# A decoder step's FFN on Trainium2: the first two pairs of gate/up feature tiles without combined products, slice roles, and the place of one down weight

## The chip, the cores and the metric

The kernel runs on one core of a Trainium2 chip. The metric is the device time of one execution in microseconds (us), the median over several runs. The engines are named as in the profile: PE (TensorE), DVE (VectorE), ACT (ScalarE), POOL (GpSimd) and SP (the queue that issues most of the DMAs).

## The reference, cut to what matters

The reference is one inference step of a two-layer decoder: an mLSTM layer, then an attention layer, each followed by a SwiGLU FFN. The change is inside the FFN, which runs twice (once a layer):

```python
def swiglu(xn, w_gu, w_d):
    gu = xn @ w_gu
    return (jax.nn.silu(gu[..., :D_FF]) * gu[..., D_FF:]) @ w_d

h = h + swiglu(rmsnorm(h, prm['norm_ffn'][l]), prm['w_gate_up'][l], prm['w_down'][l])
```

`D_MODEL` is 1024 and `D_FF` is 2816. There are 1104 tokens (64 of the sample group, 16 meta tokens and 1024 of the prompt); both groups use the same weights. All inputs are float32.

## The kernel before, in words

**Precision.** Each float32 operand is split into a high and a low part (`hi` by a cast on ACT, `lo` by a subtraction on DVE; `Net.split`, L330 and L331, and the same two steps in `PairWeights.split`, L114 and L115, and in `Mix.cast` and `Mix.rest`). A product is three matmuls: hi x hi, hi x lo, lo x hi (`mm3`, or the loop at L1326).

**Token slices.** The tokens are three slices `t` = 0, 1, 2 of 336, 384 and 384 columns. Activations lie feature-major in `H[t]`: partitions are 128 features, then 8 feature blocks, then the tokens of the slice. `y(k, t)` is block pair `k` (256 features, 768 columns of 384) of slice `t`.

**Order of an FFN.** `mlp` first runs the layer's output projection, slice after slice (`unit(t, m, x)`, tiles `pops`): 24 matmuls for each of 8 output blocks, an add into `H` on DVE (L529), a square on ACT and a running sum of squares (`add_sq`, L403) on POOL or DVE, and a write of `H` to memory (`hD`). While slice 2 is projected, the slices before it are normalised (`Mix.zero` for slice 0, `Mix.one` for slice 1) and the first weights are prepared. Then `ffn` runs gate/up, then down.

**Gate/up.** The 22 tiles of 128 features of gate and up are taken two at a time as 22 `Unit(x)`: even `x` is a pair of gate tiles, odd `x` the matching pair of up tiles. A pair of feature tiles, four blocks of the contraction and three token slices would be 24 block products; the kernel makes 20, numbered `r` = 0 to 19, from sums and differences of weight blocks (`SUMS`, made on POOL by `PairWeights.sums`, L99) and of activation blocks (made once for all units from the `y(k, t)`). Each product is 6 matmuls on PE (`u.p(r, b)`, accumulating in PSUM bank `b`). Products in `PURE` (0, 2, 11, 15) have 336 columns, the others 384. Intermediate bank contents are copied out on ACT (`u.copy`, L1332) or added to or subtracted from a saved part on DVE (`u.mark`, L1306 and L1307). `u.out(c, i, t)` ends an output tile: for a gate pair a Silu on ACT (L1348), kept in place; for an up pair a multiply with the kept tile on DVE (L1345) and a write to memory (`hT`, L1346, issued on SP). The parts are called `s1`, `c15`, `s2`, `e`, `t4`, `v2`; `fs` gives each two places, for even and odd units; `swap` exchanges two pairs of places in every second even unit, because a kept gate tile is still needed while the next gate pair begins. A unit's last four products (19, 14, 6, 3) are issued inside the next unit, interleaved with its first ones (`steps(u, v)`), so product 6 of unit `x` marks the same place of each following unit.

Raw weights come in by `weights.load(x)` (L75, on SP), one unit's pair at a time. Sums for unit `x + 1` are made while unit `x` runs.

**The first unit** (`x` = 0) is written out by hand in `ffn` from L1459 on: its products stand between the steps that normalise slice 2 (`m.root(2)`: a matmul of the sums of squares and a square root; `m.inverse(2)`: three reciprocals; `scaled` on DVE, `times` on POOL) and combine the slices (`m.add`, `m.sub` on DVE or, with `True`, on POOL; `m.cast` and `m.rest` into the operand tiles). Its raw weights and some sums lie in the `ny` tile, its sums are made during slice 2's projection.

**Who sets the order.** Inside `manual_schedule` the named engines keep program order: PE always, DVE and ACT too from slice 2's projection to L1566 and again from the last gate/up unit on (L1583). POOL and SP are ordered by the framework's planner, as are DVE and ACT in the steady units.

**Down.** The chunks `seq` go over slice `t`, half `z` of the output and 11 pairs `c` of hidden tiles, with 24 matmuls each (`dps`). Each chunk needs a weight block (`w_load(i)`, L1450, 512 KB into one of three places, `slots[0]`, `slots[1]` and `wr`, in turn; `w_split(i)`) and, for `z` = 0, a hidden block (`h_load(j)`, L1433, on POOL; `h_split(j)`). `wr` belongs to a pool that is opened only when the gate/up pool is closed. `H` itself is reloaded from `hD` by L1647.

Of the kernel before, what the change touches and what calls it, by code (L numbers as in the profile page):

```python
# [7 lines left out]
F32 = mybir.dt.float32  # L8
# [38 lines left out]
BLOCKS = ((17, 15, 18, 10), (8, 2, 9, 13), (12, 5, 1, 4), (11, 0, 14, 7), (6, 3))  # L47
SAME = {16: 4, 19: 14}
STAGED = (15, 18, 10, 2, 9, 13, 12, 5, 1, 4, 11, 0, 14, 6)
# [3 lines left out]
        (5, (1, 0), (1, 1), 1), (4, (1, 2), (1, 3), 1), (11, 9, (0, 3), -1), (0, (0, 1), (1, 1), -1), (14, (0, 2), (0, 3), 1),  # L53
        (6, (0, 0), (0, 1), 1))
# [3 lines left out]
class PairWeights:  # L58
# [3 lines left out]
    def __init__(self, net, w, slots, H, first):  # L62
        self.net, self.w, self.H, self.first, self.slots = net, w, H, first, slots
        self.both = [(slots[2 + g], slots[LOW[g]]) for g in range(4)]
        self.at = {r: (g, i) for g, b in enumerate(BLOCKS) for i, r in enumerate(b)}

    def raw(self, x, f, k, n=1):
        at, o = ((self.first, 0), (self.H[0], 0), (self.H[1], 0))[0 if x == 0 else 1 + x % 2]
        o += f * KT * P + k * 2 * P
        return at[:, o : o + n * 2 * P]  # L70
# [6 lines left out]

    def place(self, r, n=1, low=True):
        g, i = self.at[r]
        return self.both[g][low][:, i * 2 * P : (i + n) * 2 * P]  # L80

    def staged(self, x, r):
        last = (4, 11, 0, 6, 14, 5)
        if x == 0 and r in (1, 3):
            return (self.first, 8) if r == 1 else (self.slots[1], 3)
        i = last.index(r) if x == 0 and r in last else STAGED.index(r)
        return (self.slots[i // 4], i % 4) if i < 8 else (self.H[2], i - 8)

    def source(self, x, r, n=1):
        if isinstance(r, tuple):  # L90
            return self.raw(x, *r)
        if r in SINGLE and (x or r != 3):
            return self.raw(x, *SINGLE[r])
        t, i = self.staged(x, r)
        return t[:, i * 2 * P : (i + n) * 2 * P]

    def sums(self, x, part=slice(None)):
        for o, a, b, s in SUMS[part]:
            self.net.nc.gpsimd.tensor_tensor(out=self.source(x, o), in0=self.source(x, a), in1=self.source(x, b),  # L99
                                             op=ALU.add if s > 0 else ALU.subtract)  # L100

    def split(self, x, g, only=None):
        runs = []
        for r in BLOCKS[g]:
            if only and r not in only:
                continue
            at = self.staged(x, r) if r in STAGED else None
            if at and runs and runs[-1][2] and runs[-1][2][0] is at[0] and runs[-1][2][1] + runs[-1][1] == at[1]                     and self.at[runs[-1][0]][1] + runs[-1][1] == self.at[r][1]:
# [3 lines left out]
        for r, n, _ in runs:  # L112
            hi, lo, src = self.place(r, n, False), self.place(r, n), self.source(x, r, n)
            self.net.nc.scalar.copy(hi, src)  # L114
            self.net.nc.vector.tensor_tensor(out=lo, in0=src, in1=hi.bitcast(F32), op=ALU.subtract)  # L115
# [5 lines left out]
class Mix:  # L121
# [3 lines left out]
    def __init__(self, net, H, g, pp):  # L125
        self.net, self.nc, self.H, self.g, self.pp = net, net.nc, H, g, pp
        self.X = {}
# [43 lines left out]
    def gained(self, t, k):  # L171
        y = self.H[t][:, k, : TS[t][1] - TS[t][0]]
        self.nc.scalar.activation(y, y, AF.Copy, scale=self.net.gain[:, self.g + k : self.g + k + 1])

    def times(self, t, k):
        y = self.y(k, t, self.n)
        self.nc.gpsimd.tensor_tensor(out=y, in0=y, in1=self.r.unsqueeze(1).broadcast_to([P, 2, self.n]), op=ALU.mult)
# [5 lines left out]
    def zero(self, two):  # L183
# [3 lines left out]
        v = [t[:, : 2 * n].rearrange("p (k n) -> p k n", k=2) for t in two]  # L187
# [4 lines left out]
        self.places(self.net.new_x(0), PURE)  # L192
        for k in (2, 1, 3, 0):
            self.scaled(0, k)
            yield
            if k == 2:
                self.cast(15, y(2))
            elif k == 1:
                self.add(v[0], y(1), y(2))
                self.cast(0, v[0])  # L200
                self.rest(15, y(2))
            elif k == 3:
                self.cast(11, y(3))
                self.rest(0, v[0])
            else:
                self.add(v[1], y(0), y(3))
                self.cast(2, v[1])
            yield
        self.rest(11, y(3))
        self.rest(2, v[1])  # L210

    def one(self):
# [4 lines left out]
        self.places(self.net.new_x(1), (4, 14, 13, 3))  # L217
        self.scaled(1, 2)
        yield
        self.scaled(1, 3)  # L220
        self.cast(4, y(2, 1))
        self.scaled(1, 1)
        self.cast(14, y(3, 1))
        self.scaled(1, 0)
        yield
        self.rest(4, y(2, 1))
        self.sub(y(1, 0), y(1, 1), y(1, 0))
        self.sub(y(2, 0), y(1, 0), y(2, 0))
        yield
        self.rest(14, y(3, 1))  # L230
        self.cast(13, y(2, 0))
        self.sub(y(2, 1), y(2, 1), y(3, 1))
        self.add(y(3, 1), y(2, 0), y(2, 1))
        self.cast(3, y(3, 1))
        yield
        self.rest(13, y(2, 0))
        self.sub(y(2, 0), y(0, 1), y(0, 0), True)
        yield
        self.rest(3, y(3, 1))
        self.sub(y(3, 1), y(2, 0), y(3, 0), True)  # L240
        self.sub(y(2, 1), y(3, 1), y(2, 1), True)


class Net:
# [219 lines left out]
    def mlp(self, H, w, l, heads=None, cb=None):  # L464
# [8 lines left out]
        with self.pool(self.uid("nsp")) as sp, self.pool(self.uid("npp"), bufs=2, space=PSUM) as pn:  # L473
# [26 lines left out]
            with ExitStack() as c:  # L500
# [24 lines left out]
                def unit(t, m, x):  # L525
# [4 lines left out]
                    self.add_sq(H, t, m, sp, x, KT - 1 if t < 2 else KT - 2)  # L530
                    (nc.sync if t == 2 else nc.gpsimd).dma_start(self.hD[:, m, TS[t][0] : TS[t][1]], H[t][:, m])

                weights = PairWeights(self, self.I["w_gate_up"][l], slots, flat, nyt.rearrange("p x k n -> p (x k n)"))
# [2054 lines left out]
```

## Time and profile before

| | |
|---|---|
| median of 3 runs | 3036.09 us (3033.24 to 3036.29) |
| profiled execution: time, span | 3033.08 us, 3031.4 us |
| mean granted PE clock | 0.976 |
| busy share of the span | PE 94%, DVE 57%, ACT 43%, POOL 37% |
| gate/up of layer 0: first matmul of unit 0 to last of unit 21 | 577.65 to 1083.15 us |
| gate/up of layer 1 | 2228.35 to 2732.17 us |

A row of a timeline gives the start in us from the span's start, the duration in us, the engine, the line of the kernel, the operation, `output<-inputs` by tile names, the shape, and in brackets the idle time of that engine before it and what ended the idle time. `x3` means that three such instructions in a row were merged. Matmul durations overlap, since a matmul is issued before the one ahead of it has ended: how fast PE works is seen from the distance of their starts. In a row of waits, the numbers are the total in us, how often, and the longest. In layer 0 the tiles of `H` appear as `vA`, in layer 1 as `Ht`; the twelve-odd tiles called `slot` hold raw weights, sums and split weights in turn.

### The profile page before, as it was taken

The numbers are of one execution on the slowest core, as the hardware profiler recorded it, in microseconds if no ns is written. First come the engines' busy times: TensorE is split into PE (matmuls) and PEld (weight loads), VectorE is DVE, ScalarE is ACT, GpSimd is POOL, SyncE is SP. The second block draws the span as 40 slices with busy tenths as digits, with TensorE's granted clock in tenths as the row PEclk, the third lists the DMA queues.
The fourth block names the chain that finished last, engine by engine and source line by source line (L and its number), as shares of the span: only waits on it lengthen the run. The fifth ranks groups of instructions, "written<-read, shape, count | busy, mean of one in ns | idle before, by whom it ended". The sixth has DMA issues, their size and how long they took to land.

```text
span 3031.4 us, 53802 instructions
## 1 busy us (share of the span) xinstructions
PE 2836.8 (94%) x20446; PEld 2694.8 (89%) x20446; DVE 1721.3 (57%) x3462; ACT 1314.0 (43%) x2627; POOL 1117.5 (37%) x1644
## 2 busy tenths in 40 slices
PE   7999988789999989999999999999969999998999
PEld 7998878779999989999999887676968999998998
DVE  5032555877776745463355443776487667764543
ACT  5122453344444434342344444777234444443432
POOL 2011224565655511104353101544447565631110
PEclk9999999899999999999999999999989999999999
DMA  7052535122222266544443675442412222226653
GB/s 219 15 128 81 138 101 190 43 78 79 74 74 74 88 222 209 182 142 149 132 165 133 229 273 210 135 144 81 152 52 70 73 80 79 74 86 228 207 186 105
DMA packets 300142, 392.81 MB, mean 130 GB/s; under 512 B 32238, under 2 KB 222698, under 8 KB 298858
## 3 DMA queue, kind: packets, MB, share of 16 engines
q1 hardware_dynamic: 262978, 270.05, 27.5%
q0 software_dynamic: 33232, 117.01, 11.7%
q8 instruction: 161, 2.64, 0.4%
q10 hardware_dynamic: 3672, 2.31, 0.3%
q14 instruction: 99, 0.81, 0.1%
HBM read 292.19 MB, written 97.10 MB: 128 GB/s over the span
## 4 chain that ended last, share of the span: by engine, by line
PE 63%; DVE 14%; ACT 5%; issue 4%; DMA 3%; POOL 1%; DVEq 0%; ACTq 0%; POOLq 0%; SPq 0%
PE m L1326 21%; PE dps L261 6%; PE dps L260 6%; PE dps L262 6%; PE tmps L260 3%; PE tmps L261 3%; PE tmps L262 3%; DVE slot L115 2%; PE sp L2375 1%; PE op L2462 1%; DVE s L2379 1%; PE pops L262 1%; PE pops L260 1%; PE pops L261 1%; ACT slot L114 1%
## 5 line engine op out<-in xcount | busy, mean ns | idle before, releaser
L1326 PE MATMUL m<-x2h,slot 128*128 128x384 f32 x704 | 205.2, 342 | 27.5 <-ACT x2h L140 23.6
L1326 PE MATMUL m<-x0h,slot 128*128 128x336 f32 x704 | 186.2, 319 | 1.1 <-ACT vA L1332 0.5
L331 DVE TENSOR_TENSOR slot<-slot,slot 128x1024 fp32r<-128x1024 f32 x96 | 123.2, 1288 | 100.6 <-ACT slot L330 100.4
L115 DVE TENSOR_TENSOR slot<-slot,slot 128x512 fp32r<-128x512 f32 (+2 forms) x184 | 142.3, 780 | 53.4 <-ACT slot L114 47.9
L403 POOL TENSOR_TENSOR ns<-ns,nq 128x384 f32<-128x384 f32 (+1 forms) x70 | 77.8, 1111 | 235.7 <-ACT nq L401 234.2
L330 ACT CAST slot<-slot 128x1024 fp32r<-128x1024 f32 x96 | 100.8, 1052 | 144.7 <-PE dps L261 105.6
L1326 PE MATMUL m<-x1h,slot 128*128 128x384 f32 x528 | 158.8, 341 | 0.4 <-DVE vA L529 0.4
L1326 PEld LDWEIGHTS m<-x2h,slot 128*128 128x128 f32 x704 | 131.4, 191 | 30.2 <-ACT x2h L140 24.2
L114 ACT CAST slot<-slot 128x512 fp32r<-128x512 f32 (+2 forms) x184 | 111.5, 614 | 103.2 <-PE m L1326 95.3
L115 DVE TENSOR_TENSOR slot<-Ht,slot 128x256 fp32r<-128x256 f32 (+2 forms) x105 | 91.3, 870 | 83.1 <-ACT slot L114 83.1
L115 DVE TENSOR_TENSOR slot<-vA,slot 128x256 fp32r<-128x256 f32 (+2 forms) x105 | 90.2, 860 | 83.7 <-ACT slot L114 83.7
L1433 POOL DMA_DIRECT2D hr<-hT x60 | 32.6, 543 | 275.5 <-DVE T_2l L331 75.5
L1326 PEld LDWEIGHTS m<-x0h,slot 128*128 128x128 f32 x704 | 125.9, 189 | 2.8 <-ACT c L1332 1.1
L99 POOL TENSOR_TENSOR slot<-vA 128x256 f32<-128x256 f32 x105 | 92.7, 899 | 90.4 <-DMA vA<-in_w_gate_up 88.5
L99 POOL TENSOR_TENSOR slot<-Ht 128x256 f32<-128x256 f32 x105 | 91.3, 886 | 92.2 <-DMA Ht<-in_w_gate_up 90.2
L1326 PE MATMUL m<-T_2h,slot 128*128 128x384 f32 x352 | 107.9, 347 | 17.9 <-ACT fs L1332 5.1
L1326 PE MATMUL m<-x2l,slot 128*128 128x384 f32 x352 | 120.0, 341 | 3.6 <-DVE x2l L136 3.6
L1326 PE MATMUL m<-T_4h,slot 128*128 128x384 f32 x352 | 108.2, 348 | 9.6 <-DVE Ht L1306 5.0
L1326 PE MATMUL m<-x0l,slot 128*128 128x336 f32 x352 | 112.0, 318 | 0.0
L331 DVE TENSOR_TENSOR slot<-wr,slot 128x1024 fp32r<-128x1024 f32 x44 | 56.7, 1289 | 80.1 <-ACT slot L330 77.1
L1326 PEld LDWEIGHTS m<-x1h,slot 128*128 128x128 f32 x528 | 98.5, 190 | 1.5 <-issue 0.7
L2402 ACT ACTIVATE s<-s,nb 128x272 f32<-128x272 f32 (+7 forms) x126 | 99.1, 788 | 0.0
(803 smaller groups left out, 10353.6 us busy)
## 6 DMA issues: line engine op xcount, KB each, us to landing
slot<-in_w_down SPq DMA_DIRECT2D x88, 512.0 KB
wr<-in_w_down SPq DMA_DIRECT2D x44, 512.0 KB
vA<-in_w_gate_up SPq DMA_DIRECT2D x42, 512.0 KB
Ht<-in_w_gate_up SPq DMA_DIRECT2D x42, 512.0 KB
hr<-hT POOLq DMA_DIRECT2D x46, 384.0 KB, 5.1
kp<-in_cache_k SPq DMA_DIRECT2D x32, 512.0 KB
vp<-in_cache_v SPq DMA_DIRECT2D x32, 512.0 KB
wraw<-in_w_in_a SPq DMA_DIRECT2D x24, 512.0 KB
```

The source lines that it names most:

```text
L99: self.net.nc.gpsimd.tensor_tensor(out=self.source(x, o), in0=self.source(x, a), in1=self.source(x, b), op=ALU.add if s > 0 else ALU.subtract)
L114: self.net.nc.scalar.copy(hi, src)
L115: self.net.nc.vector.tensor_tensor(out=lo, in0=src, in1=hi.bitcast(F32), op=ALU.subtract)
L260: mm(ps, sh, mh, start=first, stop=False)
L261: mm(ps, sh, ml, start=False, stop=False)
L262: mm(ps, sl, mh, start=False, stop=last)
L330: self.nc.scalar.copy(hi, src)
L331: self.nc.vector.tensor_tensor(out=lo, in0=src, in1=hi.bitcast(F32), op=ALU.subtract)
L403: (nc.vector if x >= late else nc.gpsimd).tensor_tensor(out=s, in0=s, in1=sq, op=ALU.add)
L1326: nc.tensor.matmul(u.b[b][:, :n], w[p][:, k], x[q][:, k], start=new and k == i == 0, stop=k == 1 and i == 2, skip_group_check=True)
L1433: nc.gpsimd.dma_start(hraw[j], hT[t][:, 2 * c : 2 * c + 2])
L2402: nc.scalar.activation(ss[z, u], ss[z, u], AF.Exp, bias=nb[:, z : z + 1], accum_out=sm[:, u, z : z + 1])
```

## The change

- **Two pairs plainly.** Units 0 and 1 (the first gate pair and its up pair) are no longer combined. `direct(x, t)` makes the two feature tiles of one pair and one slice by 2 x 8 x 3 plain matmuls, in the order (0, 0), (1, 0), (0, 1), (0, 2), (1, 1), (1, 2) of `(x, t)`. Their raw weights lie in `slots[0]` and `slots[1]` and are split whole (`plain_split`) during slice 2's projection. The combined units begin with `x` = 2, which so has no predecessor `v`.
- **Combinations behind them, without GpSimd.** `Mix.zero`, `Mix.one` and the hand-written part make the normalised slices first, then the sums and differences, all on DVE and ACT; `times` moves from POOL to DVE, and so do slice 2's sums of squares (`late` becomes 1). `load(2)` and `sums(2)` come when the combinations of slice 0 are done, since the raw weights overwrite it; `load(3)` later.
- **Slice roles.** `s2` and `e`, `s1` and `t4` exchange the slices 1 and 2 that they end in (`out`). `swap` becomes `turn`, a rotation of `s2`, `v2`, `e`, `t4` over four even units. `out("t4", ...)` moves behind the first `c15` mark.
- **Sums.** Two pairs of adds (5 and 4, 6 and 14) become one POOL instruction each, of 128 x 512.
- **Third raw down weight.** Chunk 2's raw weight goes to `flat[1]`, where the raw weights of unit 21 lay, and is loaded in unit 21's second step; `wr` is used from chunk 5 on.

```diff
-BLOCKS = ((17, 15, 18, 10), (8, 2, 9, 13), (12, 5, 1, 4), (11, 0, 14, 7), (6, 3))
+BLOCKS = ((17, 15, 18, 10), (8, 2, 9, 13), (12, 1, 5, 4), (14, 0, 11, 7), (6, 3))
...
-        (5, (1, 0), (1, 1), 1), (4, (1, 2), (1, 3), 1), (11, 9, (0, 3), -1), (0, (0, 1), (1, 1), -1), (14, (0, 2), (0, 3), 1),
-        (6, (0, 0), (0, 1), 1))
+        ((5, 4), 1), (11, 9, (0, 3), -1), (0, (0, 1), (1, 1), -1), ((6, 14), 0))
...
+    def plain_split(self, x, f):
+        self.net.split(self.raw(x, f, 0, 4), *self.plain(x, f))
...
     def times(self, t, k):
         y = self.y(k, t, self.n)
-        self.nc.gpsimd.tensor_tensor(out=y, in0=y, in1=self.r.unsqueeze(1).broadcast_to([P, 2, self.n]), op=ALU.mult)
+        self.nc.vector.tensor_tensor(out=y, in0=y, in1=self.r.unsqueeze(1).broadcast_to([P, 2, self.n]), op=ALU.mult)
...
-                    self.add_sq(H, t, m, sp, x, KT - 1 if t < 2 else KT - 2)
+                    self.add_sq(H, t, m, sp, x, KT - 1 if t < 2 else 1)
...
+                    if x > 1:
+                        mix.gained(2, rows[x - 2])
+                    if x in (2, 3):
+                        weights.plain_split(0, x - 2)
                     if x == 3:
...
+                        weights.load(1)
+                    if x in (5, 7):
+                        weights.plain_split(1, (x - 5) // 2)
...
-        swap = {"s2": "v2", "v2": "s2", "e": "t4", "t4": "e"}
+        turn = {"s2": "v2", "v2": "e", "e": "t4", "t4": "s2"}
...
-                u.at = {(swap.get(c, c) if x % 4 == 2 else c): p[x % 2] for c, *p in fs}
+                u.at = {}
+                for c in fs:
+                    o = c
+                    for _ in range(0 if u.odd else x // 2 % 4):
+                        o = turn.get(o, o)
+                    u.at[c] = fs[o][x % 2]
...
                 u.mark("t4", sub, 3, "t4")
-                u.out("t4", 1, 1)
                 u.p(11, 0)
                 u.mark("c15", add, 0, "c15", z)
+                u.out("t4", 1, 2)
...
-                wraw[i] = view((self.slots[0], self.slots[1], wr if i > 1 else None)[i % 3])
+                wraw[i] = view((self.slots[0], self.slots[1], wr if i > 2 else flat[1])[i % 3] if i > 1 else self.slots[i])
...
+        def direct(x, t):
+            n, ends = size[t], []
+            for f in range(2):
+                w = [a.rearrange("p (k n) -> p k n", k=KT) for a in weights.plain(x, f)]
+                b = bank("mp", "d")[:, :n]
+                for j in range(KT):
+                    k = 2 * (ks if t == 2 else (2, 1, 3, 0))[j // 2] + j % 2
+                    a = [z[:, k % 2] for z in m.X[m.D[t][k // 2]]]
+                    self.mm3(b, w[0][:, k], w[1][:, k], a[0], a[1], j == 0, j == KT - 1)
+
+                def evict(b=b, o=spare[t][f][:, :n], f=f):
+                    if x:
+                        tt(out=o, in0=b, in1=o, op=ALU.mult)
+                        nc.sync.dma_start(hT[t][:, f], o)
+                    else:
+                        nc.scalar.activation(o, b, AF.Silu)
+                ends.append(evict)
+            return ends
...
+        ends = direct(0, 0)
...
         m.root(2)
...
+        for evict in ends:
+            evict()
         m.inverse(2)
...
+        ends = direct(1, 0)
+        for i, k in enumerate(ks):
+            (m.scaled if k == last else m.times)(2, k)
+            m.cast_block(2, k)
+            if i:
+                m.rest_block(2, ks[i - 1])
+            if i == 2:
+                ends[0]()
+        m.rest_block(2, last)
+        ends[1]()
...
+        ends = direct(0, 1)
...
+        m.rest(9, y(0, 0), -1.0)
+        m.rest(13, y(2, 0), -1.0)
+        ends[1]()
         weights.load(2)
...
+        ends = direct(0, 2)
...
+        weights.sums(2)
...
+        ends = direct(1, 1)
+        weights.split(2, 0)
+        for evict in ends:
+            evict()
+        ends = direct(1, 2)
...
+        weights.load(3)
+        weights.split(2, 1)
+        ends[0]()
+        m.rest(19, y(3, 1))
+        weights.split(2, 4)
+        weights.split(2, 2)
+        ends[1]()
+        weights.sums(3, slice(0, 9))
         order.close()
         with fixed():
             v = None
-            for x in range(1, NF - 1):
+            for x in range(2, NF - 1):
...
                 if g == 1:
+                    w_load(2)
                     w_split(0)
...
-            for i in range(2, 5):
+            for i in range(3, 5):
                 w_load(i)
```

321 lines of the change are left out of this document (127 added, 194 removed).

## The prediction

> **What bounds the kernel now.** I read the page first, then the waits of TensorE over the whole span, then windows, timelines and the chain of waits around the places that these named.
>
> ```profile
> PE 2836.8 (94%) x20446; PEld 2694.8 (89%) x20446; DVE 1721.3 (57%) x3462; ACT 1314.0 (43%) x2627; POOL 1117.5 (37%) x1644
> PE m L1326 <- ACT x2h L140: 23.6, 2, 11.8
> PE dps L260 <- ACT x0h L330: 17.5, 2, 9.6
> PE nps L156 <- DVE ns L403: 14.8, 2, 8.1
> ```
>
> TensorE is the bound, and its three longest waits (us in total, times, longest) come once in each of the two layers' FFNs. Two are in the prelude, from the last output-projection matmul of token slice 2 (`pops`) into the gate/up units; one is at the start of the down projection. The prelude of layer 0:
>
> ```profile
> 576.87 0.34 PE L262 MATMUL pops<-x2h,wo 128*128 128x384 f32 x1
> 580.00:590.00 10.00, 2.01 (x4) 1.40 (x5) 7.32 (x10) 5.01 (x12) 4.64 (x3) 0.69 0.11 39
> 590.00:600.00 10.00, 5.97 (x23) 4.71 (x22) 9.87 (x10) 2.72 (x6) 4.30 (x2) 0.80 0.00 0
> 600.00:610.00 10.00, 0.69 (x1) 0.29 (x1) 9.83 (x7) 1.66 (x3) 7.51 (x3) 0.54 0.00 0
> 610.00:620.00 10.00, 8.62 (x32) 8.12 (x33) 6.64 (x8) 4.80 (x9) 1.20 (x2) 0.61 0.61 172
> 683.57 0.34 PE L1326 MATMUL m<-U_6h,wl0h 128*128 128x384 f32 x1
> 1044.18 0.34 PE L1326 MATMUL m<-U_6h,wl0h 128*128 128x384 f32 x1
> 2228.18 0.34 PE L262 MATMUL pops<-x2h,wo 128*128 128x384 f32 x1
> 2332.47 0.33 PE L1326 MATMUL m<-U_6h,wl1h 128*128 128x384 f32 x1
> ```
>
> Window columns are PE, PEld, DVE, ACT, POOL busy, granted clock, DMA share, GB/s. From 580 to 610 VectorE works 27 of 30 us and TensorE 9, and the granted clock falls to 0.54: slice 2's sum, norm and combinations are a serial DVE/POOL chain. The `U_6h` rows mark product 6 of the third unit, executed inside the fourth. So pops end (576.87+0.34) to that mark takes 106.4 us in layer 0 and 104.0 in layer 1. Seventeen units from 683.57 to 1044.18 take 21.2 us each.
>
> **Part 1, the first two pairs plainly.** What must TensorE do at least? The pitch of matmuls:
>
> ```profile
> 527.14 0.31 PE L262 MATMUL pops<-x0h,slot 128*128 128x336 f32 x1
> 529.92 0.32 PE L262 MATMUL pops<-x0h,slot 128*128 128x336 f32 x1
> 574.97 0.34 PE L260 MATMUL pops<-x2h,wo 128*128 128x384 f32 x1
> 576.87 0.34 PE L262 MATMUL pops<-x2h,wo 128*128 128x384 f32 x1
> ```
>
> Eighteen pitches of 336 columns lie between the first two rows (0.155 us each), eleven of 384 between the others (0.173). A combined unit has 20 products of 6 matmuls; a plain unit has 2 features x 3 slices x 8 x 3 = 144, 24 more, all of 336 columns. That costs 24 x 0.155 = 3.7 us, 14.9 us for four units in the two layers. To the mark the new kernel must issue: 288 plain matmuls (96 x 0.155 + 192 x 0.173 = 48.1), the third unit without a predecessor's tail (72 x 0.173 + 24 x 0.155 = 16.2), and seven products of the fourth (36 x 0.173 + 6 x 0.155 = 7.2): 71.5 us. Without stalls that is 34.9 and 32.5 us less than before.
>
> Which stalls remain? The plain order asks for slice 0, 0, 1, then 2, so slice 2's norm has 14.9+8.3 us of matmuls ahead of it. The chain on VectorE:
>
> ```profile
> 590.72 2.58 DVE L163 RECIPROCAL nr<-nr 128x128 f32<-128x128 f32 x3
> 593.43 4.30 POOL L177 TENSOR_TENSOR vA<-vA,nr 128x768 f32<-128x768 f32 x2 [8.71 <-issue]
> 596.09 2.45 DVE L133 TENSOR_TENSOR vA<-vA,vA 128x768 f32<-128x768 f32 x1
> 599.63 0.96 DVE L136 TENSOR_TENSOR vA<-vA,vA 128x768 f32<-128x768 f32 x1
> L331 DVE TENSOR_TENSOR slot<-slot,slot 128x1024 fp32r<-128x1024 f32 x96 | 123.2, 1288 | 100.6 <-ACT slot L330 100.4
> 612.55 26.34 SPq L75 DMA_DIRECT2D vA<-in_w_gate_up  x6
> 616.57 0.73 POOL L99 TENSOR_TENSOR slot<-vA 128x256 f32<-128x256 f32 x1 [7.50 <-DMA vA<-in_w_gate_up]
> 630.91 0.91 POOL L99 TENSOR_TENSOR vA<-slot,vA 128x256 f32<-128x256 f32 x1
> ```
>
> A 768-wide operation beside a GpSimd one took 2.45 us, without one 0.96. GpSimd's multiplies, subtractions and sums of squares move to VectorE, so the lengthening goes. In the slice-2 pass VectorE has about 11 768-wide operations, three reciprocals, four weight splits (1.29 each) and 15 evictions and sums of half a microsecond (0.55 in part 2's first row): 29 us beside 33 us of matmuls (192 x 0.173). I cost it at nothing: 7.4 us of slice 0's plain matmuls now stand between pops end and the root; with the old lag, the 8.1 us of the `nps` row, 0.7 would be left. After the root (about 9 us behind pops end: 7.4 of plain matmuls, root and square root) come the reciprocals (2.6), 20 operations of 768 at 0.92, and some 2 us of scaling and evictions before `load(2)` may overwrite slice 0: about 34 us behind pops end. In the old trace the fourteen sums ended 19.3 us after the load's issue (612.55 to 631.82), so the third unit's weights are whole at 53. TensorE arrives at 49. `split(2, 4)` needs the last sum and stands ahead of the unit's first eviction on ACT; TensorE has two products before it needs that eviction, and the splits take 2 more: a stall of about 5 us. With the root's matmul and a copy not covered by a tail, 7 us a layer. Bounds 3 (sums in 10 us) and 12 (chain 15% longer): 34.9 + 32.5 - 14 = **53 us gained** (43 to 61). `load(1)`, queued on SP behind an output write, holds later `hD` writes only, which nobody awaits; its splits stand on DVE ahead of later evictions, with three `po` buffers of slack.
>
> [...]
>
> **Part 2, slice roles and order of evictions.**
>
> ```profile
> 709.38 0.55 DVE L1345 TENSOR_TENSOR vA<-vA,vA 128x384 f32<-128x384 f32 x1
> 709.96 0.82 ACT L1332 COPY vA<-m 128x384 f32<-128x384 f32 x2 [0.59 <-DVE vA L1345]
> 710.50 0.44 PE L1326 MATMUL m<-T_2h,slot 128*128 128x384 f32 x1 [0.42 <-ACT vA L1332]
> 739.36 1.08 DVE L1345 TENSOR_TENSOR nr<-nr,vA 128x384 f32<-128x384 f32 x1
> 740.37 0.49 DVE L1306 TENSOR_TENSOR vA<-m,vA 128x336 f32<-128x336 f32 x1
> 740.91 0.45 PE L1326 MATMUL m<-T_4h,slot 128*128 128x384 f32 x1 [0.42 <-DVE vA L1306]
> ```
>
> Each steady unit has one idle of 0.42 us: in even units the `t4` copy awaits the multiply that frees its place, in odd ones product 19 awaits the `c15` add behind the `t4` multiply. The four-place rotation gives `t4` the place of the old `s2`, freed one multiply earlier; `out("t4")` goes behind the `c15` add. Nineteen units x 0.42 x 2 layers = 16; next late would be another copy, so I take **13** (-5 to 16). The fused adds (two of 128x512 for four of 128x256) do the same elements on a queue that runs ahead: nothing.
>
> **Part 3, the third raw down weight.**
>
> ```profile
> 1070.57 0.76 DVE L115 TENSOR_TENSOR wl0l<-vA,wl0h 128x256 fp32r<-128x256 f32 x2
> 1084.80 11.82 DMA wr<-in_w_down
> 1090.00:1095.00 5.00, 0.56 (x4) 0.28 (x2) 0.00 (x0) 0.00 (x0) 0.00 (x0) 1.00 1.03 407
> 1096.69 1.05 ACT L330 CAST slot<-wr 128x1024 fp32r<-128x1024 f32 x1 [18.43 <-DMA wr<-in_w_down]
> 1098.44 0.65 PE L260 MATMUL dps<-x0h,slot 128*128 128x336 f32 x1 [7.89 <-ACT x0h L330]
> 1100.00:1105.00 5.00, 5.00 (x18) 5.00 (x19) 4.86 (x6) 3.30 (x4) 1.46 (x2) 0.50 0.76 240
> 2733.82 13.51 DMA wr<-in_w_down
> slot<-in_w_down SPq DMA_DIRECT2D x10, 512.0 KB
> vA<-hD POOLq DMA_DIRECT2D x2, 1536.0 KB, 9.1
> ```
>
> The load into `wr` starts at 1084.80, takes 11.8 us at 407 GB/s of other traffic, and the next `x0h` cast stands behind it on ACT. Its new place in `flat[1]` is dead when the last splits end (1071.3), 13 us earlier. TensorE wins the two waits, 7.9 + 9.6, and about 2 us each of slow clock (18 matmuls in 5 us where 32 fit, 0.50 granted): 21.5. What is late next: five weight loads of 0.52 MB and three reloads of up to 1.57 MB, some 7 MB, compete from about 1080 on; at 407 GB/s that takes 17 us, and chunk 4 starts at about 1098 (four chunks of 24 x 0.155 behind 1083). So just in time; I take **21** (5 to 25).
>
> **The sum.** Span 3031.4, profiled execution 3033.1; minus 53 + 13 + 21 = 87 gives 2946. The runs' median, 3036.1, is 3 us above that execution, so 2949 is forecast.
>
> **The rivals.**
> Late weights (0.12): the chain to `load(2)`, SP's order and the sums leave some 12 us more per layer than I allow, cold clock included: 2949 + 24 = 2973. For: the third unit's load comes late of necessity. Against: 27 us of DVE saturation contained lengthened operations.
> Down stays DMA-bound (0.08): the writes and reloads at 407 GB/s move the wait to chunk 4: 16 of 21 lost, 2965.
> The fused adds hold VectorE (0.06): 1.46 instead of 0.73 us at a time would cost about half a microsecond in each of 40 units: 2969. The 2.45 us row speaks for it; the few tenths of slack at each copy bound it. [...]
> Slower (0.06): GpSimd becomes the bound, because its two strided double adds run far slower than their elements. Ten singles at 0.9 take 9 us; with T for each double, a unit lasts 9 + 2T, and 87 us over 40 units is 2.2 us on the forecast's 20.8, so it decides from 9 + 2T = 23, T = 7; at T = 7.5 a unit takes 24 and the time is 2949 + 40 x 3.2 = 3077. Against: the 768-wide GpSimd row does 2.15 us each.
> No effect (0.02): plain matmuls eat what the waits give, 3036.
>
> **How the numbers follow.** The forecast has 0.66. A measurement of this kernel tells 0.2%, 6 us, from no change. Faster are the forecast and the first three rivals: 0.92; same 0.02; slower 0.06. The best ends (61 + 16 + 25) give 2934; all three low ends together (43, -5, 5) would give 2993, but hardly come at once, and 43, 5 and 10 give 2978, which takes in the first three rivals. Range 2934 to 2978.
>
> **What would show it.** Right: no `nps` wait over 2 us on TensorE, no `x2h` wait of 11.8; granted clock 1.00 through the prelude; pops end to the fourth unit's `U_6h` about 78 us; one wait of 3 to 7 us at the third unit's second or third product, released by ACT; steady units 20.8 us; the first `x0h` wait gone. Wrong: an idle of over 8 us in the third unit, steady units over 21.2, or a `dps` wait on `in_w_down`.

## The result, and the profile after

The changed kernel takes 2948.02 us (median of 4 runs, 2946.11 to 2959.27), the kernel before, run beside it, 3035.09 (3033.24 to 3036.29): a ratio of 0.9721, 95% interval 0.9696 to 0.9746. Forecast were 2949 us, with a range of 2934 to 2978. The total came out; its terms did not, and they missed in both directions.

The profiled execution of the changed kernel is the longest of its four (2959.27 us, span 2957.4): its first output projection begins 10.5 us later than in the profile of before, in code that the change leaves alone, and its other three runs took 2946.1 to 2948.7 us. So the stages below are compared with each other, not the spans.

First the engines' totals and TensorE's longest waits in the gate/up units (us in total, times, longest), from the page and from the view of waits over the whole span:

```profile
PE 2836.6 (96%) x20542; PEld 2711.6 (92%) x20542; DVE 1708.2 (58%) x3406; ACT 1305.3 (44%) x2591; POOL 999.5 (34%) x1480
PE m L1331 <- DVE Ht L1306: 5.7, 1, 5.7
PE m L1331 <- DVE vA L1306: 5.3, 1, 5.3
PE m L1331 <- ACT ns L1337: 4.4, 5, 2.0
...
PE nps L417 <- DVE ns L409: 0.2, 1, 0.2
```

The three waits that led the list before (23.6, 17.5 and 14.8 us) are gone: there is no `dps` row any more, and `nps` has 0.2 us in the down stage. New at the top are two waits for VectorE (L1306, additions into an eviction place; `vA` is layer 0, `Ht` layer 1). TensorE is busy for the same 2837 us with 96 matmuls more, in a shorter span.

The timeline rows that bound the stages, layer 0 and then layer 1: last `pops`, product 6 of the third unit (now the row with `T_1h,wl`, since the tile of that combination changed), and the same product 18 units later:

```profile
586.94 0.34 PE L268 MATMUL pops<-x2h,wo 128*128 128x384 f32 x1
673.12 0.34 PE L1331 MATMUL m<-T_1h,wl0h 128*128 128x384 f32 x1
1045.30 0.34 PE L1331 MATMUL m<-T_1h,wl0h 128*128 128x384 f32 x1
2195.98 0.34 PE L268 MATMUL pops<-x2h,wo 128*128 128x384 f32 x1
2281.13 0.34 PE L1331 MATMUL m<-T_1h,wl1h 128*128 128x384 f32 x1
2653.56 0.33 PE L1331 MATMUL m<-T_1h,wl1h 128*128 128x384 f32 x1
```

| us | before | after | gained | forecast |
|---|---|---|---|---|
| prelude (last `pops` to product 6), layer 0 / 1 | 106.4 / 104.0 | 85.8 / 84.8 | 39.7 | 53 |
| steady unit, mean of 18 | 21.21 / 21.22 | 20.68 / 20.69 | 19.2 | 13 |
| down (last gate/up matmul to last `dps`) | 279.4 / 287.5 | 267.3 / 274.6 | 25.0 | 21 |
| sum | | | 83.9 | 87 |

The late start costs 10.5 us and the stages between differ by less than 3 us each; that leaves 74.0 between the spans, 3031.4 and 2957.4. For the prelude, the windows of layer 0 (PE, PEld, DVE, ACT, POOL busy, granted clock, DMA share, GB/s), its two waits besides the 5.3 us above, and VectorE's timeline ahead of that longest one:

```profile
600.00:610.00 10.00, 10.00 (x61) 10.00 (x60) 9.90 (x14) 5.89 (x9) 0.00 (x0) 1.00 0.05 17
...
635.00:640.00 5.00, 2.99 (x18) 2.71 (x17) 5.00 (x6) 4.16 (x8) 4.59 (x5) 1.00 0.37 107
640.00:645.00 5.00, 3.44 (x18) 3.12 (x18) 5.00 (x6) 2.29 (x6) 5.00 (x6) 1.00 0.43 132
645.00:650.00 5.00, 3.46 (x12) 3.04 (x12) 5.00 (x6) 1.20 (x3) 4.92 (x4) 0.66 0.53 159
650.00:655.00 5.00, 0.87 (x3) 0.87 (x4) 5.00 (x6) 0.44 (x1) 5.00 (x5) 0.78 0.00 1
655.00:660.00 5.00, 5.00 (x18) 5.00 (x17) 1.70 (x3) 0.62 (x1) 3.17 (x5) 0.54 0.00 0
660.00:665.00 5.00, 5.00 (x32) 5.00 (x31) 3.36 (x7) 2.52 (x6) 1.11 (x1) 1.00 0.00 0
```

```profile
PE m L1331 <- ACT ns L1337: 2.0, 1, 2.0
PE m L1331 <- ACT vA L1337: 1.9, 1, 1.9
```

```profile
644.85 0.47 ACT L1337 COPY vA<-m 128x384 f32<-128x384 f32 x1
645.11 1.48 DVE L154 SCALAR_TENSOR_TENSOR x2l<-vA,x2h 128x768 fp32r<-128x768 f32 x1
646.51 0.54 DVE L1484 TENSOR_TENSOR fs<-mp,fs 128x384 f32<-128x384 f32 x1
646.98 1.02 DVE L337 TENSOR_TENSOR slot<-vA,slot 128x768 fp32r<-128x768 f32 x1
647.92 2.03 DVE L154 SCALAR_TENSOR_TENSOR x2l<-vA,x2h 128x768 fp32r<-128x768 f32 x1
649.87 0.94 DVE L337 TENSOR_TENSOR slot<-vA,slot 128x256 fp32r<-128x256 f32 x1
650.73 1.47 DVE L337 TENSOR_TENSOR slot<-slot,slot 128x768 fp32r<-128x768 f32 x1
652.13 1.48 DVE L337 TENSOR_TENSOR slot<-vA,slot 128x256 fp32r<-128x256 f32 x1
653.53 0.55 DVE L1306 TENSOR_TENSOR vA<-m,vA 128x384 f32<-128x384 f32 x1
654.13 0.69 PE L1331 MATMUL m<-U_6h,slot 128*128 128x384 f32 x1 [5.30 <-DVE vA L1306]
```

From 590 to 635 TensorE is full (one window of it is shown) at clock 1.00: the plain products do cover slice 2's norm, although VectorE is busy for 19.9 of the 20 us from 600 to 620. The trouble begins where the third unit starts, at 635.87. VectorE is busy for 5.00 of 5 us in four windows, GpSimd (the fourth unit's sums) beside it. The copy into `e` ends on ScalarE at 645.3; the addition into `e`, on which product 13 waits, runs at 653.53, behind two rests (L154: products 7 and 3), one eviction of the plain part and four splits, two of them the fourth unit's. All that work is needed later than the addition. Meanwhile the granted clock falls to 0.54: 18 matmuls in the window 655 to 660 against 32 in the next, at 1.00.

### The profile page after: what moved, and what is told of

It is laid out like the page before. It is cut to its first block, busy times and chain, and to the rows that moved or that the text cites. A ratio compares the mean times of both kernels' runs of the same rounds, so it can differ in the third digit from the quotient of the medians.

```text
span 2957.4 us, 53672 instructions
## 1 busy us (share of the span) xinstructions
PE 2836.6 (96%) x20542; PEld 2711.6 (92%) x20542; DVE 1708.2 (58%) x3406; ACT 1305.3 (44%) x2591; POOL 999.5 (34%) x1480
## 4 chain that ended last, share of the span: by engine, by line
PE 70%; DVE 9%; ACT 4%; issue 4%; DMA 2%; POOL 1%; DVEq 0%; ACTq 0%; POOLq 0%; SPq 0%
PE m L1331 24%; PE dps L266 6%; PE dps L268 6%; PE dps L267 6%; PE tmps L266 3%; PE tmps L267 3%; PE tmps L268 3%; PE pops L268 2%; PE pops L266 2%; PE pops L267 2%; PE sp L2380 1%; DVE slot L337 1%; PE op L2467 1%; DVE s L2384 1%; PE bps L266 1%
## 5 line engine op out<-in xcount | busy, mean ns | idle before, releaser
L337 DVE TENSOR_TENSOR slot<-slot,slot 128x1024 fp32r<-128x1024 f32 (+3 forms) x264 | 270.5, 1027 | 131.8 <-ACT slot L336 125.4
L336 ACT CAST slot<-slot 128x1024 fp32r<-128x1024 f32 (+3 forms) x264 | 208.0, 790 | 249.1 <-PE dps L267 92.4
L1331 PE MATMUL m<-x2h,slot 128*128 128x384 f32 x480 | 135.5, 337 | 0.0
L337 DVE TENSOR_TENSOR slot<-Ht,slot 128x256 fp32r<-128x256 f32 (+3 forms) x101 | 85.3, 846 | 63.9 <-ACT slot L336 63.9
L337 DVE TENSOR_TENSOR slot<-vA,slot 128x256 fp32r<-128x256 f32 (+3 forms) x101 | 85.4, 847 | 63.4 <-ACT slot L336 63.4
L1331 PE MATMUL m<-x1l,slot 128*128 128x384 f32 x320 | 107.5, 336 | 0.0
L2442 ACT COPY th<-tp 128x768 f32<-128x768 f32 (+1 forms) x80 | 73.4, 919 | 53.8 <-PE tp L2434 30.8
L108 POOL TENSOR_TENSOR Ht<-Ht 128x512 f32<-128x512 f32 (+1 forms) x60 | 85.3, 1422 | 29.3 <-DVE wl1l L337 29.3
L108 POOL TENSOR_TENSOR vA<-vA 128x512 f32<-128x512 f32 (+1 forms) x60 | 85.4, 1424 | 28.4 <-DVE wl0l L337 28.4
L1834 DVE TENSOR_REDUCE ss<-sqb 128x4 f32<-128x256 f32 (+1 forms) x72 | 30.2, 419 | 101.8 <-ACT sqb L1833 101.0
```

The lines of the kernel that those rows point to most:

```text
L108: self.net.nc.gpsimd.tensor_tensor(out=o, in0=a, in1=b, op=op)
L336: self.nc.scalar.copy(hi, src)
L337: self.nc.vector.tensor_tensor(out=lo, in0=src, in1=hi.bitcast(F32), op=ALU.subtract)
L1331: nc.tensor.matmul(u.b[b][:, :n], w[p][:, k], x[q][:, k], start=new and k == i == 0, stop=k == 1 and i == 2, skip_group_check=True)
L1834: nc.vector.tensor_reduce(out=ss[:m, i, :], in_=sq[:m].rearrange("p (h d) -> p h d", d=DH), op=ALU.add, axis=AX.X)
L2442: nc.scalar.copy(th.rearrange("p x z (u h q) -> p h (x z u) q", h=2, q=64)[:, :, :n], pt[:, :, :n])
```

## The experiments

Prelude, steady unit and down are those of the table above, as layer 0 / layer 1; ratios are to the kernel before, with the 95% interval.

**The third weight alone.** The kernel before with part 3 only:

```
-wraw[i] = view((self.slots[0], self.slots[1], wr if i > 1 else None)[i % 3])
+wraw[i] = view((self.slots[0], self.slots[1], wr if i > 2 else flat[1])[i % 3] if i > 1 else self.slots[i])
...
+                    w_load(2)
                     w_split(0)
```

> The kernel before with part 3 alone: chunk 2's raw down weight in the dead place, loaded in the last unit. Theory A (the wait for that one load was the whole loss at the start of down, and nothing takes its place): the dps waits of 7.9 and 9.6 us go, and the stretch from the last gate/up matmul to the last of down is shorter by 12 to 13 us in each layer, as between the two profiles: 23 to 26 us off, about 3010. Rival B (the reloads keep the queues full, and the whole change only got its 25 us because gate/up ended otherwise): a dps wait on in_w_down comes back at chunk 4, under 10 us off.

Measured: 3011.37 us, ratio 0.9902 (0.9874 to 0.9931). Down takes 267.29 / 274.62 us, which is 12.1 and 12.9 less than before and the value of the full change to 0.02 us; prelude (108.7 / 104.9) and steady unit (21.23) gain nothing. Part 3 is worth 25 us by itself, with nothing late behind it (as whole kernels the medians differ by 31.6 us, and the runs of either scatter by 10 to 15):

```profile
1095.00:1100.00 5.00, 5.00 (x34) 5.00 (x33) 0.77 (x1) 1.71 (x2) 1.17 (x2) 1.00 1.03 388
```

The DMA engines are as full as before (1.03, 388 GB/s), but TensorE stays busy beside them at clock 1.00.

**The rotation and the order of evictions.** Three kernels built on the kernel before: both edits of part 2, then each alone.

```
-u.at = {(swap.get(c, c) if x % 4 == 2 else c): p[x % 2] for c, *p in fs}
+# even units: places of s2, v2, e, t4 turned x//2 % 4 times
...
-u.out("t4", 1, 1)
 u.p(11, 0)
 u.mark("c15", add, 0, "c15", z)
+u.out("t4", 1, 1)
```

> The kernel before with part 2 alone: the four-place rotation and out(t4) behind the c15 add, old slice roles. Theory A (each of the 0.42 us idles costs 0.69 us of pitch, since the first matmuls behind an idle start later): the steady unit falls from 21.2 to about 20.6 us, 19 units in two layers: 19 to 24 us off. A2 (an idle costs just its 0.42): 16 off. Rival B (another copy becomes late at once, and only one kind of unit gains): 8 to 10 off.

> The kernel before with the rotation over four places alone: the multiply that ends t4 stays directly behind its mark. In this kernel that place decides the queue: the odd units' c15 add stands behind the multiply on VectorE, unlike in e2. Theory A, two waits with two causes: the even units' wait goes with the rotation, the odd units' wait for the c15 add stays at 0.42 us of idle and about 0.7 us of pitch in every second unit: steady unit 20.85 (before 21.21, e2 20.50). Rival B, the rotation also makes the multiply shorter or earlier, and the odd wait goes with it: 20.5. With 18 units in each layer, A gives about 13 us less than before, B 26.

> The kernel before with the t4 multiply behind the c15 add alone, and the old exchange of two places. Theory A, two waits with two causes: the odd units' wait goes; the even units' wait grows, since the multiply that frees the place of their t4 copy now runs half a microsecond later (in e8, with both the new order and the old exchange, it was 1.2 us in every second unit): steady unit about 21.2, no gain by itself. Rival B, each half is worth its own 0.35 us per unit: 20.85, 13 us less than before.

| kernel | steady unit, us | wait left, every second unit |
|---|---|---|
| before | 21.21 / 21.22 | 0.42 for the `t4` copy; 0.42 for the `c15` addition |
| rotation alone | 20.87 / 20.82 | `c15` addition |
| order alone | 20.85 / 20.80 | `t4` copy |
| both | 20.50 / 20.43 | none |

The windows over the same 360 us of steady units, for before, rotation alone, order alone and both, tell it in matmuls (x after PE's busy time):

```profile
700.00:1060.00 360.00, 352.62 (x2038) 347.14 (x2038) 255.27 (x423) 165.03 (x339) 208.48 (x232) 1.00 0.25 78
...
700.00:1060.00 360.00, 355.81 (x2070) 352.97 (x2069) 262.98 (x435) 166.57 (x345) 218.23 (x244) 1.00 0.25 78
...
700.00:1060.00 360.00, 356.22 (x2074) 353.34 (x2073) 254.17 (x430) 165.96 (x343) 212.89 (x236) 1.00 0.26 80
...
700.00:1060.00 360.00, 360.00 (x2108) 360.00 (x2107) 255.36 (x432) 172.00 (x353) 207.31 (x234) 1.00 0.26 79
```

So there were two waits with two causes, as forecast, and the edits add up: 0.34 to 0.42 us per unit each. The exchange of slice roles, which the change has beside them, was not run alone. The order alone did not make the other wait longer, against what was expected of it. Each wait has 0.42 us of idle in every second unit and costs 0.7 us of pitch there. The matmul records of before show where the rest goes: the first matmul behind a wait starts 0.58 us later than the usual pitch, of which 0.42 is the idle, and the second another 0.11. As whole kernels they measured 3012.80 us (both; ratio 0.9912, interval 0.9883 to 0.9942), 3013.39 (rotation; 0.9921, 0.9903 to 0.9938) and 3026.61 (order; 0.9968, 0.9953 to 0.9984). By the pitch, rotation and order should differ by nothing and both should be some 13 us ahead of either; the whole times don't show that, and why not isn't settled. The steady units are the direct measure.

**The halves undone in the changed kernel.** Once with `out("t4")` back behind its mark, once with the old two-place exchange:

```
-turn = {"s2": "v2", "v2": "e", "e": "t4", "t4": "s2"}
+turn = {"s2": "v2", "v2": "s2", "e": "t4", "t4": "e"}
```

> The changed kernel with the multiply that ends t4 put back directly behind its mark, ahead of the c15 adds (the rotation of four places stays). Theory A, two separate causes: the order of evictions took the odd units' wait of 0.42 us for the c15 add (product 19 waits) away, the rotation the even units'; so one wait in every second unit comes back, each at a price of about 0.7 us of pitch: the steady unit goes from 20.68 to about 21.0, and the time rises by some 12 us to 2960. Rival B, the rotation alone did both: no wait comes back, steady unit 20.7, 2948.

> The changed kernel with the old exchange of two places (s2 with v2, e with t4) in the place of the rotation over four; the order of evictions stays new. Theory A: the even units' wait of the t4 copy for the multiply that frees its place comes back, at about 0.7 us of pitch in every second unit: steady unit about 21.0, the time some 12 us up, 2960. Rival B, the later multiply of t4 is what matters for both and the rotation does nothing: steady unit 20.7, 2948. Rival C: with the multiply of t4 behind the c15 add the old exchange frees its place still later than before, and the wait gets longer than 0.42: steady unit over 21.2, 2970 or more.

The first measured 2956.03 us, ratio 0.9726 (0.971 to 0.9743), steady 20.68 / 20.71: no change. It was a poor test. VectorE's queue is planned again from the program, and in this kernel the edit moved the multiply in one unit of each layer only. The kernels above with the rotation alone and with both edits, between which it moves in every odd unit, answer the question. The second measured 2968.69 us, ratio 0.9767 (0.975 to 0.9783), steady 21.22 / 21.24. The waits in its steady units of layer 0:

```profile
PE m L1331 <- ACT vA L1337: 4.8, 4, 1.2
PE m L1331 <- ACT fs L1337: 4.4, 4, 1.2
```

Without the rotation the copies in even units wait 1.1 to 1.2 us instead of 0.42, and the whole of part 2 is lost. Why longer than in the kernel with the order alone is open: slice roles and fused additions differ between the two.

**The multiplies on GpSimd again.** The multiplies of `times` (slice 2's norm) back on GpSimd in the changed kernel (`nc.vector` to `nc.gpsimd` in one line):

> The changed kernel with the multiplies by the norm (times, slices 1 and 2) back on GpSimd. Theory A (the chain on VectorE from the root to load(2) sets when the third unit's weights come, and GpSimd takes 2.15 us where VectorE takes 0.95, and lengthens its neighbours): load(2) starts 3 to 6 us later in each layer and the time grows by 6 to 14 us. Rival B (load(2) has slack, since the third unit waits for VectorE's backlog instead): 0 to 3 us more, with the p(13) wait unchanged.

Measured: 2956.37 us, ratio 0.9715 (0.9689 to 0.974), the same as the change within its interval. The prelude is 89.5 / 87.1, that is 3.6 and 2.3 us longer; the wait for the `e` addition is 6.4 instead of 5.3, and the one for the `s1` copy 3.4 instead of 2.0. `load(2)` is issued 3.4 and 3.0 us later behind the last `pops`, as theory A had it, and the two preludes together are 5.9 us longer, just under its 6 to 14; the whole time does not resolve so much. TensorE stays full through the slice-2 pass all the same (10.00 of 10 us in each window from 590 to 620): the price is paid in the third unit, by waits on ScalarE and VectorE.

**The third unit in program order.** The changed kernel with the instructions of its first combined unit on VectorE and ScalarE kept in program order, instead of planned with the later units, and the fourth unit's splits one step later:

```
+        with fixed(E.DVE, E.Activation):
+            v = Unit(2)
+            ...
         with fixed():
-            for x in range(2, NF - 1):
+            for x in range(3, NF - 1):
```

> The changed kernel with VectorE and ACT of the third unit (x = 2) held in program order, and the splits for unit 3 one step later, so that the e add that frees product 13's bank stands ahead of the rests 7 and 3 and of the splits of unit 3. Theory A (the 5.3 and 5.7 us waits for the e add are the planner's order on VectorE): both fall under 1.5 us, the granted clock stays at 1.00, and 12 to 18 us go in the two layers. Rival B (VectorE is simply full from 631 to 655 and what is put behind comes late instead): the wait moves to a later product of the third or to the first of the fourth unit, 0 to 5 us off.

Measured: 2939.04 us (2937.27 to 2940.55), ratio 0.9665 (0.9641 to 0.9689). The prelude is 79.6 / 79.8 us, 6.2 and 5.1 less. Its waits and clock, layer 0:

```profile
PE m L1331 <- DVE vA L1306: 2.6, 2, 2.1
PE m L1331 <- DVE ns L1307: 2.1, 1, 2.1
PE m L1331 <- ACT vA L1337: 1.4, 2, 0.8
...
645.00:650.00 5.00, 4.58 (x27) 4.58 (x28) 2.84 (x6) 2.67 (x6) 1.45 (x2) 1.00 0.00 0
```

The same work in another order: 9.2 us of waits become 6.1, and in layer 0 the clock stays at 1.00, which saves the rest. So theory A held in part: the wait for the `e` addition falls from 5.3 to 2.1 us, not under 1.5, a new one of 2.1 us comes for the `s1` subtraction, as rival B had it, and 11.3 us go in the two preludes instead of 12 to 18.

**Single additions.** The same with the two fused GpSimd additions made four again:

```
-((5, 4), 1), ... ((6, 14), 0))
+(5, (1, 0), (1, 1), 1), (4, (1, 2), (1, 3), 1), ... (6, (0, 0), (0, 1), 1), (14, (0, 2), (0, 3), 1))
```

> The kernel of e4 (the third unit in program order) with its two fused GpSimd adds of 128x512 made four adds of 128x256 again; nothing else differs. Theory A, fused adds hold VectorE in small: in e4 the 768-wide rests on VectorE took 1.44 us in the steady units where the kernel with the rotation alone (single adds) took 0.96, and every second unit keeps a wait of 0.15 us for the v2 copy; with single adds the rests go back to about 0.96, the wait goes, and the steady unit goes from 20.65 to 20.45-20.50 us, so about 3 us per layer, 2932 to 2934. Rival B, the adds are only elements on a queue that runs ahead: the steady unit stays at 20.65 and the time at 2939. Rival C, two fused instructions save GpSimd time (10 us of 360 in the windows) that the third and fourth units' late sums need: the prelude gets 2 to 3 us longer per layer, 2943.

Measured: 2930.36 us (2929.62 to 2933.1), ratio 0.9642 (0.9626 to 0.9658). This is the fastest version, against 0.9721 for the change. The steady unit is 20.53 / 20.51, the last waits in the steady units go, and the prelude stays (80.0 / 78.5). VectorE's low parts of the last weight block, by their group over 700 to 1060, in the kernel with fused and with single additions:

```profile
L337 DVE TENSOR_TENSOR wl0l<-vA,wl0h 128x256 fp32r<-128x256 f32 x34 | 26.0, 767 | 0.0
...
L338 DVE TENSOR_TENSOR wl0l<-vA,wl0h 128x256 fp32r<-128x256 f32 x34 | 17.5, 517 | 0.0
```

The price of the fused additions was as expected (0.12 and 0.19 us per unit, 5.6 us in 36 units), but not its place: the 768-wide subtractions (low parts of weights, there called rests) stayed as long (1.44 us with fused, 1.50 with single additions), and these 256-wide ones got shorter. A fused addition takes 1.40 us on GpSimd over these 360 us, a single one of the same group in the kernel before 0.87. That the longer instructions beside them lengthen the 256-wide subtractions (767 instead of 517 ns) fits these numbers; the 768-wide ones do not show it.

**Two rows later.** The split of products 6 and 3 out of the prelude into the third unit's step 1:

```
-        weights.split(2, 4)
...
+                    weights.split(2, 4)
                     weights.sums(3, slice(9, None))
```

> The kernel of e4 with the split of products 6 and 3 of the third unit (block 4) moved out of the prelude, from ahead of the unit's first copies, into its step 1. Theory A: what is left of the prelude's losses in e4 (7.9 us in layer 0) hangs on casts and rests that stand ahead of the third unit's copies on ScalarE and VectorE; with this split behind them the first copies come about 1.4 us earlier and the prelude gets 1 to 3 us shorter per layer, 2934 to 2937. Rival B: the split lands between the rests and the splits of the fourth unit's first blocks, which already wait in the same step, and lengthens that wait by as much: no change, or the prelude 1 us longer, 2939 to 2941.

Measured: 2940.89 us, ratio 0.9681 (0.9661 to 0.9702); prelude 79.8 / 80.6. No change, as rival B had it: in this saturated stretch the moved work only changes who waits for it.

**Further work moved behind the additions.** Two attempts to clear the waits that were left:

```
+            v.after["c1"] = lambda: weights.split(2, 3)   # behind the s1 subtraction
+            v.after["c2"] = lambda: bring(7, y(2, 2))     # behind the s1 multiply
...
+            bring(3, y(3, 2))
+            weights.split(3, 1)
+            weights.split(3, 2)
```

> The kernel of e5 with the third unit's splits and rests in other places: the split of block 3 behind the unit's s1 subtraction instead of ahead of its e addition, the cast and rest of product 7 behind the s1 multiply instead of ahead of the s1 subtraction, the fourth unit's first split one step later, product 3's cast and rest and the two other splits behind the unit. Theory A: the two largest waits left in e5's prelude (2.0 us for the e addition behind the split of block 3, 2.4 us for the s1 subtraction behind rest 7 and the fourth unit's split) are VectorE's backlog at the wrong place, and go: the prelude gets 3 to 5 us shorter per layer (80.0 to about 76), 2921 to 2925. Rival B: VectorE has no spare time in this stretch, and the same work is late at product 7 or at the fourth unit's first product: the prelude stays at 79 to 81, 2930.

> The edit of e11, with the fourth unit's last sums and the fifth unit's weight load one step later, behind the split of block 3, which reads the places that they overwrite (in e11 they came ahead of it, so e11's third unit used wrong weights, and one more weight load stood on SP ahead of two output writes; the s1 copy waited 5.8 us for such a write). The order on SP in the prelude is now that of e5. Theory A: e5's waits of 2.0 and 2.4 us behind VectorE's backlog go, and no new one of that size comes: the prelude is 3 to 5 us shorter than e5's 80.0 and 78.5, steady 20.5, 2921 to 2925. Rival B: the load and the sums, one step later, make the fourth or the fifth unit's weights late, or product 7 waits for its rest: a new wait of 2 us or more, 2930 or above.

In both the fifth unit's sums overwrite staged sums of the fourth before they are split, so the fourth unit multiplies other weights; in the first, the third does too. The first took 2944.63 us, ratio 0.97 (0.9681 to 0.972): TensorE waited 5.8 us for its `s1` copy, which waited for an output write. The second took 2936.17 us (2925.07 to 2941.34), ratio 0.9657 (0.9635 to 0.9679), with a prelude of 80.3 / 78.5. Its waits in layer 0 are 4.7 us, where the fastest version has 6.5, but the clock was at half for 3.4 us (the last section has the rows) and took that back: the 3 to 5 us that theory A expected did not come. Whether an order that keeps the fourth unit's weights gains here is open.

## Why the prediction was right, and where its steps were not

**Part 1: the mechanism held, the stall term was half its size.** The unstalled time, 71.5 us, stands: the fastest version takes 80.0 us in layer 0, and 8.4 of the 8.5 us above it are found as lost pitch between its matmuls. The chain was placed well: `load(2)` is issued 33.6 us behind the last `pops` (34 forecast, though the terms given for it add up to 32), the last sum ends at 50.7 (53), the third unit starts at 48.6 (49).

```profile
620.91 5.51 SPq L74 DMA_DIRECT2D vA<-in_w_gate_up  x3
637.05 0.94 POOL L108 TENSOR_TENSOR vA<-vA 128x256 f32<-128x256 f32 x1
635.87 0.34 PE L1331 MATMUL m<-x1h,slot 128*128 128x384 f32 x1
638.02 0.83 ACT L336 CAST slot<-vA 128x768 fp32r<-128x768 f32 x1 [0.64 <-POOL vA L108]
```

The step that failed is "a stall of about 5 us. With the root's matmul and a copy not covered by a tail, 7 us a layer". Lost were 14.3 and 13.3 us (85.8 and 84.8 minus 71.5), that is 27.6 instead of 14, which is the whole miss of part 1: the 39.7 us gained lie below its own bounds of 43 to 61. The forecast looked for one stall on ScalarE, behind `split(2, 4)` and the last sum. A wait of 2.0 us came there, but behind the split of block 3: its cast (the last row above) had to wait 0.64 us for that sum, and the cast of product 3 stood behind it, ahead of the unit's first copy. The casts of `split(2, 4)` had run at 634.3. Two other waits followed, 1.9 us on ScalarE, whose queue stood at a cast that waited for the fourth unit's sums on GpSimd, and 5.3 us on VectorE; then about 4 us of slow matmuls (layer 0: 14.2 us of lost pitch from 586 to 670, of which 9.9 stand at the three waits and 0.4 at the start). VectorE was costed at nothing for the slice-2 pass, rightly (its terms there add up to 26.6 us, not 29, beside 33 of matmuls); but the account ended there. Rests 7 and 3, the splits of two units and a late eviction of the plain part came next, in an order planned for units that are not starved. With the third unit in program order and the fourth unit's splits a step later, 5 to 6 us a layer come back: this is shown.

**The granted clock** was forecast at 1.00 through the prelude, and was not. It was at half from 646 on, behind waits of 2.0 and 1.9 us and ahead of the 5.3 us one: at 0.50 from 645.99 to 649.41, and again from 652.82 to 659.65. The first of these stretches lasts 3.41 us; it is the last row here, and the three rows ahead of it are windows of the same length (x counts every matmul that reaches into a window):

```profile
635.75:639.16 3.41, 2.24 (x14) 1.96 (x12) 3.41 (x5) 2.77 (x5) 3.00 (x3) 1.00 0.51 148
639.16:642.58 3.42, 2.56 (x14) 2.56 (x15) 3.42 (x5) 1.93 (x5) 3.42 (x4) 1.00 0.16 58
642.58:645.99 3.41, 1.50 (x8) 1.18 (x8) 3.41 (x4) 1.51 (x3) 3.33 (x5) 1.00 0.54 154
645.99:649.41 3.42, 2.84 (x10) 2.42 (x9) 3.42 (x4) 0.88 (x2) 3.42 (x3) 0.50 0.71 211
```

The wait of 2.0 us (638.0 to 640.0) is divided between the first two windows, and the clock stays. The one of 1.9 us (643.5 to 645.4) lies whole in the third, and half clock follows. TensorE was idle for 1.91 of 3.41 us in that third window, and for 1.17 and 0.86 in the two before. The slow matmuls cost about 4 us in layer 0, where the forecast had none. Why the clock fell behind the one wait and not behind the other, longer one is not shown.

**Part 2: under-sized.** "Nineteen units x 0.42 x 2 layers = 16" took the idle for the price; a wait of 0.42 us costs 0.7 of pitch. What the two edits are worth alone is 0.71 to 0.80 us a unit, some 27 us. In the change part 2 gave 19.2, above its own bounds of -5 to 16. Of the 7.9 us between, 5.6 came back with single additions: the fused ones, costed at nothing, were not free. The cause of the other 2.3 is open.

**Part 3: 25.0 for 21.** The waits went as forecast, and nothing was late behind them; the slow clock was under-sized. The rows of before, down stage of layer 0:

```profile
PE dps L260 <- ACT x0h L330: 7.9, 1, 7.9
PE dps L261 <- DVE x0l L331: 0.7, 1, 0.7
PE nps L411 <- DVE ns L403: 0.5, 1, 0.5
```

These 9.1 us became 0.2, while the stage got 12.1 us shorter: 3.2 us are left for the slow matmuls behind the wait, where "about 2 us each" stood.

So 13 us too much in part 1 stand against 6 and 4 too little in parts 2 and 3. The total was right because the misses cancel, and that is luck: parts 1 and 2 both lie outside their own bounds. The 3 us between the 83.9 of the stages and the 87.1 of the medians lie outside these stages or in the scatter of the runs.

**The rivals.** Late weights: no, the sums were whole 2 us earlier than forecast, and of the third unit's waits only the 0.64 us of ScalarE's idle time above stand for its own weights. Down DMA-bound: no, the DMA is full (share 1.03 from 1075 to 1080) and TensorE does not wait (5.00 of 5 us busy there). GpSimd as the bound: no, a fused addition takes 1.41 us and not 7. The fused additions holding VectorE: real, at about a third of the 20 us that the rival gave it (5.6 us).

## What to carry to other kernels

When long work is put ahead of a starved stretch, do the account of every engine for the units behind it too: here VectorE had room under the plain products and none in the first unit after them, and which of its queued operations went first was worth 5 to 6 us a layer. Price a wait by the pitch it costs, from matmul start to matmul start, and not by the idle time beside it (0.7 us for an idle of 0.42 here). And an operation that is fused to save instructions on a side engine can go with longer ones on another (VectorE's 256-wide subtractions here, 767 instead of 517 ns); undo it alone before it is called free.

## What the hardware showed that was not expected

The length of a wait does not decide alone whether the clock falls. In the fastest version four waits of 0.9, 0.6, 2.0 and 2.4 us within 14 us left the granted clock at 1.00; in the last experiment two waits of 0.9 and 0.6 us were followed by half clock. The windows of the fastest version in which its waits lie, then two of the last experiment:

```profile
630.00:635.00 5.00, 4.03 (x22) 3.33 (x20) 5.00 (x7) 2.24 (x5) 4.55 (x6) 1.00 0.18 60
635.00:640.00 5.00, 2.41 (x13) 2.13 (x14) 4.79 (x6) 0.96 (x2) 4.92 (x6) 1.00 0.49 146
640.00:645.00 5.00, 4.33 (x24) 4.01 (x24) 3.48 (x4) 2.22 (x4) 5.00 (x6) 1.00 0.36 106
645.00:650.00 5.00, 3.32 (x19) 3.32 (x20) 3.20 (x5) 1.41 (x3) 1.79 (x3) 1.00 0.00 0
...
630.00:635.00 5.00, 3.49 (x16) 2.84 (x15) 5.00 (x6) 0.96 (x2) 5.00 (x6) 0.88 0.23 77
635.00:640.00 5.00, 4.92 (x23) 4.60 (x22) 1.46 (x4) 1.36 (x3) 4.22 (x6) 0.78 0.35 110
```

The same two waits stand in both, 0.9 us ahead of the product with `T_1h` and 0.6 ahead of the one with `U_9h`:

```profile
633.66 0.45 PE L1332 MATMUL m<-T_1h,slot 128*128 128x384 f32 x1 [0.95 <-ACT vA L1338]
635.54 0.44 PE L1332 MATMUL m<-U_9h,slot 128*128 128x384 f32 x1 [0.57 <-ACT vA L1338]
636.36 0.34 PE L1332 MATMUL m<-U_9l,slot 128*128 128x384 f32 x1
636.53 0.34 PE L1332 MATMUL m<-U_9h,slot 128*128 128x384 f32 x1
...
631.75 0.44 PE L1332 MATMUL m<-T_1h,slot 128*128 128x384 f32 x1 [0.94 <-ACT vA L1338]
633.64 0.58 PE L1332 MATMUL m<-U_9h,slot 128*128 128x384 f32 x1 [0.57 <-ACT vA L1338]
634.98 0.52 PE L1332 MATMUL m<-U_9l,slot 128*128 128x384 f32 x1
635.30 0.52 PE L1332 MATMUL m<-U_9h,slot 128*128 128x384 f32 x1
```

Behind them the matmuls of the last experiment start 0.32 us apart, those of the fastest version 0.17. So the same wait can cost the clock in one run and not in the next. What decides it is open.
